# Value storage by head pair, a weight reload moved behind attention, and respaced conditioning and down weights in a two-layer decoder trunk

## The chip, the cores and the metric

The kernel runs as one program on all 8 cores of one Trainium2 chip. Each core computes one batch element, and the cores exchange nothing. The time of a run is that of the slowest core, in device microseconds (us). TensorE is written PE, VectorE DVE, ScalarE ACT, GpSimd POOL and SyncE SP; "SPq" and "ACTq" in a trace are the DMA-issuing instructions of SyncE and ScalarE.

The runs come in two states here. In the slow state the cores of one die (cores 0 to 3 are one, 4 to 7 the other), or of both, show a lower granted TensorE clock in the records and the run is some per cent longer. Measures used below:

- Fast runs: those within 1.5% of the fastest run of the same kernel. A ratio sets one kernel's fast runs against the other's fast runs of the same rounds, so it is not quite the ratio of the medians that are quoted.
- Undisturbed dies: where a kernel had too few fast runs, the mean core span over all dies whose four cores had a clock of at least 0.969, against the same mean of the kernel before in the same rounds. A run that is slow because of one die still gives one such die. The spans of such dies scatter within a kernel (standard deviation 3 to 17 us), so a difference by this measure is uncertain by some 3 to 8 us (standard error).
- Stages: cuts of a trace, explained with the profile.

## The reference, cut to what matters

```python
for l in range(DEPTH):                      # 2 layers, SEQ 4096, D_MODEL 1024, D_FF 2816
    mod = silu(c) @ ada_w[l] + ada_b[l]     # "conditioning": 9 x 1024 shifts, scales, gates
    y = modulate(rmsnorm(h, ...), sh1, sc1)
    h = h + 0.5 * g1 * swiglu(y, ffn1_wg, ffn1_wu, ffn1_wd)
    y = modulate(rmsnorm(h, ...), sh2, sc2)
    proj = y @ w_in[l]                      # u, v of the gating unit; q, k, v of attention
    out_a = spatial_gating(u, v, ...)
    out_b = dilated_mixture(rope(q), rope(k), v)   # 8 heads of 64
    h = h + g2 * (concat(out_a, out_b) @ w_out[l])
    y = modulate(rmsnorm(h, ...), sh3, sc3)
    h = h + 0.5 * g3 * swiglu(y, ffn2_wg, ffn2_wu, ffn2_wd)
```

`dilated_mixture` runs three causal patterns, (window, dilation) = (128, 1), (512, 4) and (2048, 16). For a dilation r, keys and values are taken at positions r apart, so their rows are not neighbours in memory.

## The kernel before

A sequence is cut in 8 tiles of 512 positions. Per layer the order on TensorE is: two feed-forward groups of two tiles each (gate and up matmuls, then down), projection 1 (tiles 0 to 3), two groups, with attention 1 running beside them, projection 2, output projection 1, two groups with attention 2 beside them, output projection 2, and two last groups. Everything that isn't the main line (attention, norms, conditioning, weight conversion, preparation) is a Python generator in a `Mix`. After each block of main matmuls `tick` adds its estimated nanoseconds to every generator's account, and each generator adds instructions until its own yields have used that account. So a yield of 5500.0 means "one piece per 5.5 us of main work". `drain` puts what is left of a generator into the program at once.

The background is thus interleaved when the program is built, into one list for each engine. The trace shows the result: from 1590.8 to 1603.5 us on core 4, in output projection 1, groups of 8 or 16 output-projection matmuls (L1326) alternate with groups of 8 of attention (L1173, L1202). SyncE's list alone is sorted once more, by the time at which a transfer's buffers are expected to be ready.

```python
class Mix:
    def tick(self, ns):
        for s in list(self.sides):
            s[1] += ns
            s[1] = min(s[1], 12000.0)
            while s[1] > 0 and s in self.sides:
                try:
                    s[1] -= next(s[0])
                except StopIteration:
                    self.sides.remove(s)
# ... cut ...
    def order_sp(self):
        for _, _, deps, fn, key in sorted(self.spq, key=lambda x: x[:2]):   # (ready, program order)
# ... cut ...
        def ada_gen(lo, cols, cost):            # conditioning, one 128-wide column of ada_w per piece
            ring = Zone(lo, B1).ring(8, [128, KC, 128], BF16, "ada")
            # ... cut ...
            for i, col in enumerate(cols):
                if i + n - 1 < len(cols):
                    load(i + n - 1)             # 256 KB by GpSimd's queue
                # ... cut ...
                ada_mm(ap, b, col)
                # ... cut ...
                yield cost
# ... cut ...
        def norm_load(t, src, bsrc):            # the residual tile, in four pieces
            for q in range(4):
                Sx.dma("sp", "h%d" % q, lambda e, q=q: e.dma_start(out=hbuf[0][:, 2 * q:2 * q + 2], in_=src[t, :, 2 * q:2 * q + 2]),
                       reads=bsrc[t][2 * q:2 * q + 2], writes=hbuf[1][2 * q:2 * q + 2])
# ... cut: projection, a value tile is stored ...
                vdst = bass.AP(vS.tensor, vS.offset + r0 * VW, [[VW, 16], [16 * VW, 8], [1, VW]])   # VW = 768: 1536 bytes
                Sx.dma("act", "va%d" % n, lambda e: e.dma_start(
                    out=vdst, in_=va.rearrange("p a c -> p (a c)")), reads=[bva], ...)
# ... cut: attention, the values of head pair p at dilation r ...
            def load_v(p, r):
                if r == 1:
                    # ... one DMA: 128 x 16 or 17 rows of 192 values (384 bytes) ...
                    return
                v, b = ax.v4 if r == 4 else ax.v16
                st_ = 128 * r
                n0 = -1 if sbi else 0
                for n in range(n0, SB // st_):
                    src = bass.AP(vS.tensor, vS.offset + (T0 + n * st_) * VW + p * 192,
                                  [[r * VW, 128], [VW, r], [1, 192]])
                    Sx.dma("sp", "av%d" % r, lambda e, n=n, src=src: e.dma_start(out=v[:, (n + 1) * r:(n + 2) * r, :], in_=src), ...)
# ... cut: output projection, the norm of a finished tile ...
                    def fin(sq=sq, t=t, n=n):
                        # ... cut ...
                        yield from norm_mods(1800.0, yv[ym[n // 2]], l, 2, t)
                        if n == 0:
                            norm_load(tiles[2], hS, bHS)
# ... cut: main line, projection 1 to output projection 1 ...
            side["at"] = mix.add(attn_gen(0, 1950.0))
            ffn_group(l, 0, (4, 5), src, bsrc, FB4, nxt=[f1(6), f1(7)])
            side["late"] = False
            def mid1(p, k):
                nonlocal mx
                if p == "down" and k == 4:
                    mix.drain(side["at"])                # the rest of attention 1, at once
                    mx = side["mx"] = MX()
                    # ... rope tables ...
                    side["win"] = mix.add(win_again(l, mx, 2200.0))   # projection weights again
            # ... cut ...
            ffn_group(l, 0, (6, 7), src, bsrc, FB4, posts=posts, hook=mid1)
            mix.drain(side["win"])
            project(4, False)
            # ... cut ...
            side["at"] = attn_gen(1, 2000.0)
```

The softmax here doesn't subtract the row's maximum and nothing guards it: scores larger than these inputs give would overflow.

## Time and profile before

Six runs of the kernel before gave a median of 5517.65 us (5323.34 to 6093.05), slow ones among them.

I cut the trace at the first matmul of each stage: gate (L733), down (L779), projection (L941), output projection (L1326 before, L1319 after). Attention is L1173 and L1202 before, L1166 and L1195 after. The matmuls that sum squares for a norm are L621. G is a gate stage and D a down stage with the group's number (8 groups in a layer), P a projection, O an output projection; P1 is the projection that follows group 1, O3 the output projection that comes after group 3 and projection P3. An undisturbed gate stage takes 152 us, a down stage 76 and an output projection 58 to 59. The first lines of the profile's page, which is of the slowest core:

```profile
span 5324.4 us, 84020 instructions; the slowest of 8 cores (5276.9 to 5324.4 us)
...
PE 4982.1 (94%) x27826; PEld 2323.7 (44%) x27826; DVE 2298.2 (43%) x4018; ACT 1895.3 (36%) x2879; POOL 664.4 (12%) x705
...
DMA packets 420054, 875.29 MB, mean 164 GB/s; under 512 B 154640, under 2 KB 187792, under 8 KB 412432
...
PE 75%; DMA 10%; ACT 6%; DVE 3%; issue 3%; SPq 2%; POOL 1%; ACTq 0%; DVEq 0%; POOLq 0%
```

TensorE is busy 94% of the span, and the chain that ended last (the last line) is 75% TensorE. So the kernel is near its bound, and what is left is a set of local stalls. They are seen in the windows of core 4, below in the order G0, D0, G1, D1, P1, D3 (the down stage that ends attention 1), O3 (output projection 1), O13 (output projection 2 of layer 1). The columns are the stage's start and end, its length, busy time and instructions of each engine, granted TensorE clock, share of the 16 DMA engines' time that was busy, and what they moved.

```profile
core 4: us, PE busy (x) PEld busy (x) DVE busy (x) ACT busy (x) POOL busy (x), PEclk, DMA share, GB/s
49.20:239.40 190.20, 174.72 (x961) 78.25 (x962) 73.40 (x112) 58.32 (x92) 29.61 (x56) 0.95 0.88 157
239.40:362.60 123.20, 87.72 (x474) 39.04 (x473) 18.64 (x28) 12.28 (x19) 16.94 (x32) 0.86 1.02 222
362.60:521.20 158.60, 155.31 (x802) 70.91 (x801) 62.98 (x97) 28.31 (x47) 15.33 (x29) 1.00 0.92 211
521.20:602.00 80.80, 79.71 (x369) 35.95 (x368) 22.50 (x33) 21.97 (x36) 2.64 (x5) 1.00 0.85 224
602.00:761.90 159.90, 152.57 (x738) 69.63 (x737) 105.93 (x301) 79.90 (x150) 92.97 (x74) 0.98 0.52 152
1235.70:1357.70 122.00, 91.65 (x492) 42.70 (x490) 32.17 (x51) 26.27 (x40) 11.72 (x12) 0.86 0.71 198
1519.80:1603.40 83.60, 66.90 (x377) 30.55 (x377) 38.48 (x57) 33.87 (x49) 0.20 (x1) 0.90 0.96 291
...
4760.70:4819.90 59.20, 58.86 (x274) 26.54 (x273) 33.87 (x49) 23.60 (x36) 0.00 (x0) 1.00 0.83 260
```

D0 is 47 us longer than an undisturbed down stage, with PE idle for 35.5 us (123.20 less 87.72) while the DMA engines are full (1.02). In G0 the DMA share is 0.88 and PE is busy for 174.7 of 190.2 us, so that stage has some DMA room. D3 has 30 us without a matmul, at a clock of 0.86. O3 has 16.7 us.

The waits of PE on core 4 say for what it stood still: us in all, number of times, longest.

```profile
PE ps L621 <- ACT arena L613: 74.7, 12, 18.2
...
PE ps L779 <- DMA arena<-wdS: 60.2, 5, 23.9
...
PE ps L733 <- DVE arena L792: 9.1, 2, 8.4
```

The first line is the norm of a residual tile that arrives late (L613 squares the tile's elements); one of its waits is in O3. The second is down weights, and its longest wait is in D3. The chain of work through O3 (start, us, what) shows why the tile was late there:

```profile
1536.45 0.32 SPq L1104
1537.07 0.59 SPq L1115
1537.76 10.96 SPq L1123
...
1562.92 7.36 DMA arena<-hS
1570.45 0.76 DVE arena L1334
1571.29 0.64 ACT arena L613
```

SyncE issues the K load of attention 2 (L1104), the dilation-1 value load (L1115) and then the first dilated one (L1123), and that one issue takes 10.96 us. Stores and the residual tile stand behind it in SyncE's list: the seven dilated loads take 19.79 us to issue, the next store goes at 1557.7 and the tile's load at 1562.9. All dilated value loads, and the value stores, in the trace of core 4 (issue duration in ns: least, median, most):

```profile
L1123 SPq DMA_DIRECT2D arena<-vS x96: 523/631/10964, 763.1 to 4552.1; - x96
...
L1043 ACTq DMA_DIRECT2D vS<-arena x64: 525/525/3777, 632.4 to 4112.7; - x64
```

### The profile page before, as it was taken

To read this page: it belongs to the slowest core of one execution; us is meant where nothing else is said; L and a number is where in the kernel's file an instruction comes from. 1 tells how busy PE (TensorE), PEld (TensorE's weight loads), DVE (VectorE), ACT (ScalarE), POOL (GpSimd) and SP (SyncE) were. 2 spreads that over 40 slices of the span, in tenths; PEclk is the share of its full clock that TensorE was granted. 3 is DMA by queue.
4 is the path that set the end of the run, shared out by engine and by line. 5 is a ranking of instruction groups with operands and counts; after the bars stand their busy time and mean duration, and the time that the engine had idled before them with its cause. 6 is when DMAs were issued, how large, how long until landed. Compare 5 with 4: busy or idle time off the path is not lost.

```text
span 5324.4 us, 84020 instructions; the slowest of 8 cores (5276.9 to 5324.4 us)
## 1 busy us (share of the span) xinstructions
PE 4982.1 (94%) x27826; PEld 2323.7 (44%) x27826; DVE 2298.2 (43%) x4018; ACT 1895.3 (36%) x2879; POOL 664.4 (12%) x705
## 2 busy tenths in 40 slices
PE   5969999998889999898999999999989999999998
PEld 2434444444334444344444444444444444444443
DVE  2313365443455544332333335544536544535342
ACT  2211253553334543112122313455424454513321
POOL 1110250011320011010100003300005000000000
PEclk9989999999999999899999999999999999999999
DMA  9898754644686554868676644546354736468331
GB/s 169 159 217 202 190 164 120 196 115 121 185 218 187 161 168 118 243 155 207 146 198 171 185 147 128 141 127 185 100 184 134 247 101 200 158 192 262 109 106 59
DMA packets 420054, 875.29 MB, mean 164 GB/s; under 512 B 154640, under 2 KB 187792, under 8 KB 412432
## 3 DMA queue, kind: packets, MB, share of 16 engines
q1 hardware_dynamic: 305392, 600.51, 36.1%
q0 software_dynamic: 40512, 139.35, 16.4%
q10 hardware_dynamic: 73728, 130.06, 7.6%
q8 instruction: 234, 3.83, 0.3%
q14 instruction: 188, 1.54, 0.1%
HBM read 821.94 MB, written 239.08 MB: 199 GB/s over the span
## 4 chain that ended last, share of the span: by engine, by line
PE 75%; DMA 10%; ACT 6%; DVE 3%; issue 3%; SPq 2%; POOL 1%; ACTq 0%; DVEq 0%; POOLq 0%
PE ps L733 42%; PE ps L779 18%; PE ps L941 6%; PE ps L1326 3%; PE ps L1202 3%; PE ps L1173 2%; DMA arena<-wd 2%; PE ps L621 2%; DMA arena<-wdS 1%; DMA arena<-wgu 1%; DMA hS<-arena 1%; DMA arena<-hS 1%; DMA arena<-xP 1%; POOL arena L1023 1%; DVE arena L1013 1%
## 5 line engine op out<-in xcount | busy, mean ns | idle before, releaser
L733 PE MATMUL ps<-arena 128*128 128x512 bf16 x11264 | 2568.8, 381 | 36.5 <-DMA arena<-wgu 11.4
L733 PEld LDWEIGHTS ps<-arena 128*128 128x128 bf16 x11264 | 1066.0, 98 | 1269.0 <-issue 75.2
L779 PE MATMUL ps<-arena 128*128 128x512 bf16 x5632 | 1289.8, 385 | 96.2 <-DMA arena<-wdS 50.1
L741 DVE SCALAR_TENSOR_TENSOR arena<-arena,ps 128x512 f32<-128x512 f32 x704 | 482.5, 685 | 1063.0 <-ACT arena L738 1047.0
L738 ACT ACTIVATE arena<-ps 128x512 f32<-128x512 f32 x704 | 419.3, 597 | 1429.2 <-PE ps L733 1187.6
L779 PEld LDWEIGHTS ps<-arena 128*128 128x128 bf16 x5632 | 543.7, 99 | 741.6 <-issue 135.2
L743 DVE TENSOR_TENSOR arena<-ps,arena 128x512 bf16<-128x512 f32 x704 | 486.8, 691 | 292.9 <-PE ps L733 256.5
L792 DVE SCALAR_TENSOR_TENSOR arena<-ps,arena 128x512 f32<-128x512 f32 x256 | 192.0, 750 | 945.3 <-PE ps L779 628.6
L941 PE MATMUL ps<-arena 128*128 128x512 bf16 x2560 | 579.8, 384 | 19.8 <-DVE arena L1013 16.7
L1180 ACT ACTIVATE arena<-ps 128x1024 bf16<-128x1024 f32 (+1 forms) x384 | 358.4, 933 | 382.0 <-PE ps L1173 357.7
L613 ACT ACTIVATE arena<-arena 128x512 bf16<-128x512 f32 x352 | 204.9, 625 | 597.1 <-DVE arena L1334 249.5
L941 PEld LDWEIGHTS ps<-arena 128*128 128x128 bf16 x2560 | 249.2, 99 | 316.4 <-issue 34.3
L645 ACT ACTIVATE arena<-arena 128x512 bf16<-128x512 f32 x384 | 257.1, 718 | 199.9 <-DVE arena L641 174.3
L1187 DVE TENSOR_TENSOR arena<-arena 128x1024 bf16<-128x1024 bf16 (+1 forms) x384 | 243.7, 635 | 125.9 <-ACT arena L1180 121.7
L641 DVE SCALAR_TENSOR_TENSOR arena<-arena,ps 128x512 f32<-128x512 f32 x384 | 263.2, 740 | 77.7 <-ACT ps L627 77.2
L1235 POOL TENSOR_TENSOR arena<-arena 64x512 bf16<-64x512 f32 x128 | 162.1, 1266 | 982.3 <-ACT arena L1231 935.8
L1023 POOL TENSOR_TENSOR arena<-arena 128x512 bf16<-128x512 f32 x128 | 226.7, 1876 | 285.3 <-DVE arena L1013 285.3
L1202 PE MATMUL ps<-arena 128*128 128x128 bf16 x2736 | 218.9, 221 | 40.1 <-ACT arena L1211 26.9
L1202 PEld LDWEIGHTS ps<-arena 128*128 128x128 bf16 x2736 | 184.9, 99 | 134.5 <-issue 51.9
L1326 PE MATMUL ps<-arena 128*128 128x512 bf16 x1024 | 238.9, 386 | 1.7 <-DVE arena L1061 1.7
L621 PE MATMUL ps<-arena 128*128 128x512 bf16 x448 | 148.2, 396 | 94.2 <-ACT arena L613 80.9
L1218 DVE TENSOR_TENSOR arena<-ps,arena 128x512 f32<-128x512 f32 x256 | 176.0, 687 | 104.8 <-PE ps L1202 103.9
(65 smaller groups left out, 2040.0 us busy)
## 6 DMA issues: line engine op xcount, KB each, us to landing
arena<-wguS SPq DMA_DIRECT2D x308, 512.0 KB, 4.1
arena<-hS SPq DMA_DIRECT2D x176, 512.0 KB, 7.2
arena<-wdS SPq DMA_DIRECT2D x112, 704.0 KB, 6.1
hS<-arena ACTq DMA_DIRECT2D x224, 256.0 KB, 6.3
arena<-hS ACTq DMA_DIRECT2D x160, 256.0 KB, 6.4
wguS<-wgu POOLq DMA_DIRECT2D x66, 512.0 KB, 6.9
hS<-arena SPq DMA_DIRECT2D x128, 256.0 KB, 9.1
arena<-ada_w POOLq DMA_DIRECT2D x120, 256.0 KB, 8.9
```

What stands on the lines that cost most here:

```text
L641: Sx.op("dve", lambda e: e.scalar_tensor_tensor(out=hk, in0=hk, scalar=Av[:, b0:b0 + 1], in1=bank(nb), op0=ALU.mult, op1=ALU.mult), reads= ...
L645: Sx.op("act", lambda e: e.activation(out=out, in_=hk, func=AF.Identity, bias=modv[:, s0:s0 + 1], scale=1.0), reads=[bh, bMod[l][i]], writ ...
L733: Sx.op("pe", lambda e, kc=kc, half=half, bk=bk: e.matmul(bank(bk), lhsT=gu[:, half, kc, :], rhs=y[:, kc, :], start=(kc == 0), stop=(kc == ...
L738: Sx.op("act", lambda e: e.activation(out=sg, in_=bank(G), func=AF.Tanh, scale=0.5), reads=[psB[G]], writes=[bsg])
L741: Sx.op("dve", lambda e: e.scalar_tensor_tensor(out=sg, in0=sg, scalar=1.0, in1=bank(G), op0=ALU.add, op1=ALU.mult), reads=[psB[G]], write ...
L743: Sx.op("dve", lambda e: e.tensor_tensor(out=fx.act[s][0][:, j, :], in0=bank(U), in1=sg, op=ALU.mult), reads=[psB[U], bsg], writes=[fx.act ...
L779: Sx.op("pe", lambda e, j=j: e.matmul(bank(bk), lhsT=wd[:, j, :], rhs=act[:, j, :], start=(j == 0), stop=(j == FC - 1)), reads=[bwd, ba[j] ...
L941: Sx.op("pe", lambda e, kc=kc, lhs=lhs, rhs=rhs: e.matmul(bank(bk), lhsT=lhs, rhs=rhs, start=(kc == 0), stop=(kc == KC - 1)), reads=[bw[c ...
L1023: Sx.op("pool", lambda e, o=o, a0=a0, a1=a1, h_=h_: e.tensor_tensor(out=cust(o, 0, to), in0=cust(a0[0], 0, fr), in1=cust(a1[0], 0, fr), op ...
L1180: Sx.op("act", lambda e: e.activation(out=pv, in_=ps[:, QB:QB + 2, c0:512], func=AF.Exp, scale=0.125), reads=[psB[QB], psB[QB + 1]], write ...
L1202: Sx.op("pe", lambda e, v=v, vi=vi, h=h, b=b, pc=pc, o=o, prev=prev: e.matmul(o, lhsT=v[:, vi, h * 64:h * 64 + 128], rhs=pT[:, h, pc, b, : ...
L1326: Sx.op("pe", lambda e, kc=kc, m=m, bk=bk, mxt=mxt: e.matmul(bank(bk), lhsT=ox.w[0][:, m, kc, :], rhs=mxt[:, kc, :], start=(kc == 0), stop ...
```

## The change

The intent, in five parts:

1. Values are stored by head pair (`vS` becomes `[4, S, 192]`), so that the r rows of one residue step are one long row: 1536 bytes at dilation 4, 6144 at dilation 16. One load replaces up to five. Each value tile is then stored with four DMAs of 384-byte rows, by SyncE, where it was one of 1536-byte rows by ScalarE.
2. In output projections the third tile's residual load goes on ScalarE's queue.
3. Attention 1 is spaced more densely, and the reload of the projection weights follows it in the same stream, in place of the forced `drain` in the middle of D3.
4. Attention 2 is spaced more densely, so that it ends earlier.
5. Conditioning takes one column every 7.2 us in place of 5.5, and down weights are opened at gate step 6 in place of 11.

```diff
-VW = 768
+VW = 192
-    vS = dscr("vS", [S, VW], BF16)
+    vS = dscr("vS", [4, S, VW], BF16)
@@ norm_load
-        def norm_load(t, src, bsrc):
+        def norm_load(t, src, bsrc, eng="sp"):
-                Sx.dma("sp", "h%d" % q, ...
+                Sx.dma(eng, "h%d" % q, ...
@@ vapart
-                vdst = bass.AP(vS.tensor, vS.offset + r0 * VW, [[VW, 16], [16 * VW, 8], [1, VW]])
-                Sx.dma("act", "va%d" % n, ...
+                for p in range(4):
+                    vdst = bass.AP(vS.tensor, vS.offset + (p * S + r0) * VW, [[VW, 16], [16 * VW, 8], [1, VW]])
+                    Sx.dma("sp", "va%d" % n, lambda e, p=p, vdst=vdst: e.dma_start(out=vdst, in_=va[:, p, :]), ...
@@ load_v   (the branch for r == 1 and the loop over n are gone)
+                v, b = {1: ax.v1, 4: ax.v4, 16: ax.v16}[r]
                 n0 = -1 if sbi else 0
+                n = SB // (128 * r) - n0
+                src = bass.AP(vS.tensor, vS.offset + (p * S + T0 + n0 * 128 * r) * VW,
+                              [[r * VW, 128], [128 * r * VW, n], [1, r * VW]])
+                Sx.dma("sp", "av%d" % r, lambda e: e.dma_start(out=v[:, (n0 + 1) * r:], in_=src), ...
@@ outproj
-                            norm_load(tiles[2], hS, bHS)
+                            norm_load(tiles[2], hS, bHS, "act")
@@ early, hook0
-                yield from ada_gen(mx.lo, list(range(24, 72)), 5500.0)
+                yield from ada_gen(mx.lo, list(range(24, 72)), 7200.0)
-                if n == 11:
+                if n == 6:
                     W.open_wd(4)
@@ main line   (mid1 and the drain in it are gone)
-            side["at"] = mix.add(attn_gen(0, 1950.0))
+            def prep1():
+                # ... new MX, rope tables ...
+                yield from win_again(l, mx, 2500.0)
+            side["late"] = False
+            side["at"] = mix.add(seq(attn_gen(0, 1800.0), prep1()))
-            ffn_group(l, 0, (6, 7), src, bsrc, FB4, posts=posts, hook=mid1)
-            mix.drain(side["win"])
+            ffn_group(l, 0, (6, 7), src, bsrc, FB4, posts=posts)
+            mix.drain(side["at"])
-            side["at"] = attn_gen(1, 2000.0)
+            side["at"] = attn_gen(1, 1850.0)
```

More of the change, by code (lines that the diff above doesn't have):

```diff
@@ L596, in conv_gen @@
                 yield cost
-        def norm_load(t, src, bsrc):
+        def norm_load(t, src, bsrc, eng="sp"):
             for q in range(4):
-                Sx.dma("sp", "h%d" % q, lambda e, q=q: e.dma_start(out=hbuf[0][:, 2 * q:2 * q + 2], in_=src[t, :, 2 * q:2 * q + 2]),
+                Sx.dma(eng, "h%d" % q, lambda e, q=q: e.dma_start(out=hbuf[0][:, 2 * q:2 * q + 2], in_=src[t, :, 2 * q:2 * q + 2]),
                        reads=bsrc[t][2 * q:2 * q + 2], writes=hbuf[1][2 * q:2 * q + 2])
@@ L1041, in vapart @@
                 r0 = t * T + s * 128
-                vdst = bass.AP(vS.tensor, vS.offset + r0 * VW, [[VW, 16], [16 * VW, 8], [1, VW]])
-                Sx.dma("act", "va%d" % n, lambda e: e.dma_start(
-                    out=vdst, in_=va.rearrange("p a c -> p (a c)")), reads=[bva],
-                    writes=[bVS[t]] if s == 0 else (), accw=[bVS[t]] if s else ())
+                for p in range(4):
+                    vdst = bass.AP(vS.tensor, vS.offset + (p * S + r0) * VW, [[VW, 16], [16 * VW, 8], [1, VW]])
+                    f = s == 0 and p == 0
+                    Sx.dma("sp", "va%d" % n, lambda e, p=p, vdst=vdst: e.dma_start(out=vdst, in_=va[:, p, :]), reads=[bva],
+                           writes=[bVS[t]] if f else (), accw=() if f else [bVS[t]], ns=500.0)
                 tick(KC * MM)
@@ L1109, in load_v @@
                 rd = [bVS[t] for t in tp]
-                if r == 1:
-                    v, b = ax.v1
-                    lo = 0 if sbi else 1
-                    r0 = T0 + (lo - 1) * 128
-                    src = bass.AP(vS.tensor, vS.offset + r0 * VW + p * 192, [[VW, 128], [128 * VW, 17 - lo], [1, 192]])
-                    Sx.dma("sp", "av1", lambda e: e.dma_start(out=v[:, lo:17, :], in_=src), reads=rd, writes=[b], ns=6000.0)
-                    return
-                v, b = ax.v4 if r == 4 else ax.v16
-                st_ = 128 * r
-                n0 = -1 if sbi else 0
-                for n in range(n0, SB // st_):
-                    src = bass.AP(vS.tensor, vS.offset + (T0 + n * st_) * VW + p * 192,
-                                  [[r * VW, 128], [VW, r], [1, 192]])
-                    Sx.dma("sp", "av%d" % r, lambda e, n=n, src=src: e.dma_start(out=v[:, (n + 1) * r:(n + 2) * r, :], in_=src),
-                           reads=rd, writes=[b] if n == n0 else (), accw=() if n == n0 else [b], ns=1500.0 * r / 4)
+                v, b = {1: ax.v1, 4: ax.v4, 16: ax.v16}[r]
+                n0 = -1 if sbi else 0
+                n = SB // (128 * r) - n0
+                src = bass.AP(vS.tensor, vS.offset + (p * S + T0 + n0 * 128 * r) * VW,
+                              [[r * VW, 128], [128 * r * VW, n], [1, r * VW]])
+                Sx.dma("sp", "av%d" % r, lambda e: e.dma_start(out=v[:, (n0 + 1) * r:], in_=src), reads=rd, writes=[b],
+                       ns=4000.0)
             BACK = {1: 128, 4: 512, 16: 2048}
@@ L1482, in build_nc @@
             project(0, True)
-            side["at"] = mix.add(attn_gen(0, 1950.0))
-            ffn_group(l, 0, (4, 5), src, bsrc, FB4, nxt=[f1(6), f1(7)])
-            side["late"] = False
-            def mid1(p, k):
-                nonlocal mx
-                if p == "down" and k == 4:
-                    mix.drain(side["at"])
-                    mx = side["mx"] = MX()
-                    mx.late()
-                    side["late"] = True
-                    load_cs(mx, 4)
-                    load_cs(mx, 5)
-                    side["win"] = mix.add(win_again(l, mx, 2200.0))
+            def prep1():
+                nonlocal mx
+                mx = side["mx"] = MX()
+                mx.late()
+                side["late"] = True
+                load_cs(mx, 4)
+                load_cs(mx, 5)
+                yield from win_again(l, mx, 2500.0)
+            side["late"] = False
+            side["at"] = mix.add(seq(attn_gen(0, 1800.0), prep1()))
+            ffn_group(l, 0, (4, 5), src, bsrc, FB4, nxt=[f1(6), f1(7)])
             posts = seq(*[norm_steps(2200.0, (lambda k=k: mx.y2[k]), *p2(4 + k), gate=lambda: side["late"], lead=14000.0)
```

## The prediction

> All times are of fast runs: before takes 5324 us (the 5518 median includes slow ones).
>
> **What bounds it.** TensorE is busy 94% of the span (page part 1) and 75% of the chain of waits; the rest is local stalls. Cutting the trace at the first matmul of each gate (L733), down (L779), projection (L941) and output-projection (L1326) stage, an undisturbed gate takes 152 us, a down 76, an output projection about 58. Excess, layer 0 / layer 1:
> - start: first gate 194, first down 128 us (24, 10 and 3 us idle on wd; DMA share 1.03);
> - the down that ends attention 1: 123 / 109 us (forced attention tail 12 us, then 16 us on wdS, issued late);
> - output projection after it: 84 / 79 us (16.5 / 12.4 us idle for an hS tile queued behind value loads, one of whose issues took 10.1 / 8.2 us, timeline);
> - the down that ends attention 2: 97 / 86 us (17 / 5 us on wdS), then an output projection of 70 / 59.
> After idling, matmuls go at 427 ns instead of 215 for some us; granted clock 0.84 to 0.92 here. [...] each cured stall saves some us extra.
>
> **What the change does.**
> 1. Values: dilated loads go from 384-byte rows to 1536 and 6144; stores become 256 of 384-byte rows on SyncE instead of 64 of 1536 on ScalarE. [...] packets of 384, 1536 and 4096 bytes take 24, 79 and 205 ns, about equal per byte. So transfers save an estimated 25 us of all-engine time, less 9 for stores, none critical. Issuing counts: dilated loads cost SyncE 115 us.
> 2. Residual tile loads on ScalarE's queue, not stuck behind those. 1 and 2 together: about -12 us in each first output projection, -8 in layer 0's second.
> 3. Attention 7.5% denser, weights reloaded from its stream: no forced tail, wd less blocked: -22 and -12.
> 4. Attention 2 ends in the gate stage (instruction order), so output weights arrive earlier: -17 and -8.
> 5. Conditioning every 7.2 instead of 5.5 us: 36 instead of 44 columns used by the end of the first down (2 MB less in a DMA-bound stretch), -10; wd opened at step 6 only moves a wait. But conditioning now ends late in the second down; the order has eight norm matmuls at its end: a new stall of about 10 us before the projection.
> Costs: denser attention, more SyncE issues in projections, +5.
>
> Sum about -95: 5230 us, 1.8% faster. Range 5165 to 5285. Faster by over 2% 0.38, within 2% 0.58, slower 0.04.
>
> **What shows it.** Down ending attention 1 about 100 us; first output projections about 70; down ending attention 2 about 78; first gate plus down about 310; second down about 95 with an idle stretch before L941; packets under 512 bytes 154640 to about 101000; dilated value issues on SyncE from 115 us to under 20.
>
> **What would make it wrong.** A start deeper in DMA debt could gain much more; the win reload could still crowd wdS loads, since rope loads still wait ahead of them on SyncE; value stores could delay norm tiles in projections; the stall before the first projection could be 20 us.

Two clauses are cut from it, at the marks. No term of the sum was in them: it came to about -95 us and stays so.

## The result, and the profile after

The changed kernel took 5322.45 us in the median of 20 runs (5306.21 to 6067.06); the kernel before 5341.75 in the median of 40 (5315.85 to 6103.82). Of fast runs alone the medians are 5320.0 (13 runs) and 5325.0 (21 runs). The ratio of fast runs, computed as said above, is 0.9986, with a 95% interval of 0.9976 to 0.9996. Outputs are right. So the change is worth 0.14%, where 1.8% had been predicted, and the time lies above the predicted range.

Two lines of the page after:

```profile
span 5335.5 us, 84085 instructions; the slowest of 8 cores (5259.9 to 5335.5 us)
...
DMA packets 372951, 875.31 MB, mean 164 GB/s; under 512 B 103440, under 2 KB 137616, under 8 KB 365328
```

Bytes are the same, and a third of the packets under 512 bytes is gone: the store and load forms did change as meant. The windows of core 4 after, in the order of those before:

```profile
core 4: us, PE busy (x) PEld busy (x) DVE busy (x) ACT busy (x) POOL busy (x), PEclk, DMA share, GB/s
49.50:241.40 191.90, 174.12 (x921) 77.07 (x922) 72.92 (x111) 57.82 (x91) 26.97 (x51) 0.95 0.83 150
241.40:363.40 122.00, 87.29 (x449) 38.84 (x448) 19.15 (x29) 12.88 (x20) 15.85 (x30) 0.85 1.03 221
363.40:529.30 165.90, 160.08 (x865) 73.67 (x866) 61.33 (x92) 27.55 (x45) 19.02 (x36) 0.97 0.89 191
529.30:621.40 92.10, 82.14 (x370) 36.15 (x369) 19.87 (x30) 16.84 (x27) 5.40 (x9) 0.94 0.88 248
621.40:795.40 174.00, 156.87 (x738) 70.69 (x737) 111.00 (x308) 86.32 (x159) 90.06 (x70) 0.95 0.47 127
1273.10:1379.20 106.10, 83.28 (x404) 37.64 (x402) 24.37 (x37) 21.03 (x33) 12.54 (x13) 0.89 0.81 228
1540.60:1625.10 84.50, 68.93 (x384) 31.49 (x385) 38.77 (x57) 34.33 (x50) 0.51 (x1) 0.92 0.95 276
...
4759.00:4824.20 65.20, 60.53 (x273) 26.78 (x272) 33.76 (x49) 24.86 (x37) 0.00 (x0) 0.97 0.77 251
```

G0 and D0 are as long as before. G1, D1 and P1 are 7, 11 and 14 us longer: by the end of P1 the core is 33.5 us late (795.4 against 761.9). D3 is 16 us shorter. O3 hasn't gained. O13, which had stood still for nothing, is 6 us longer.

All stages of the span, as the mean over the six cores whose matmul records are complete in both traces (1, 2, 3, 4, 5 and 7; both runs fast), in us. Stage times of the experiments are such means too, less the mean before of this table; in four of them (two-speed conditioning, conditioning back, attention with residual, late attention) the complete cores are 0, 1, 3, 5, 6 and 7:

| stage | before | after | difference |
|---|---|---|---|
| G0 and D0 | 315.3 | 312.9 | -2.4 |
| G1 and D1 | 241.9 | 263.7 | +21.8 |
| P1 | 159.8 | 174.2 | +14.4 |
| D3 / D11 (end of attention 1, layers 0 / 1) | 120.8 / 107.4 | 103.5 / 86.2 | -17.3 / -21.3 |
| O3 / O11 (output projection 1) | 82.0 / 79.5 | 80.6 / 78.0 | -1.4 / -1.5 |
| G4, D4, G5 / G12, D12, G13 (attention 2 beside) | 473.5 / 478.5 | 482.1 / 482.5 | +8.6 / +4.0 |
| G2, D2, G3 / G10, D10, G11 (attention 1 beside) | 473.8 / 476.2 | 476.2 / 477.2 | +2.4 / +1.0 |
| D5 / D13 (end of attention 2) | 93.6 / 84.2 | 87.7 / 77.4 | -5.9 / -6.8 |
| O5 / O13 (output projection 2) | 69.2 / 59.4 | 67.5 / 65.9 | -1.7 / +6.4 |
| all other stages and the ends | | | -2.0 |
| span | 5302.9 | 5301.2 | -1.7 |

One of these six cores was disturbed: in the changed kernel's trace the clock record of core 1 stood at 0.8125 from 376.9 to 508.7 us, in its G1, which took 192.2 us (164.6 to 167.0 on the other five). With core 1 left out of both means, G1 and D1 differ by +17.8, G0 to P1 in all by +31.2, and the span by -7.7, near the 0.14%; the other rows move by 1.5 us at most.

The gain did come, and was given back: -55.9 us from D3 and D11 (-38.6), D5 and D13 (-12.7), O3 and O11 (-2.9) and O5 (-1.7); against it +33.8 at the start, +6.4 in O13 and +16.0 in the stages with attention beside them. What PE waited for after:

```profile
PE ps L621 <- ACT arena L613: 67.1, 17, 17.1
PE ps L779 <- DMA arena<-wdS: 40.1, 3, 22.8
PE ps L733 <- DVE arena L792: 26.4, 3, 11.3
```

The waits on down weights fell by 20 us, but the longest one, in D3, is there as before (22.8 us). The gate stages' wait on L792, the add of the down result to the residual, rose from 9.1 to 26.4 us. Two places show the start's loss. The end of D1 (timeline: start, us, what, and in brackets how long the engine had been idle and what ended it):

```profile
604.16 3.19 PE L779 MATMUL ps<-arena 128*128 128x512 bf16 x14
...
609.56 4.93 SPq L601 DMA_DIRECT2D arena<-hS  x4
...
615.56 1.15 ACT L613 ACTIVATE arena<-arena 128x512 bf16<-128x512 f32 x2 [1.52 <-DMA arena<-hS]
...
616.45 1.01 PE L621 MATMUL ps<-arena 128*128 128x512 bf16 x2 [9.10 <-ACT arena L613]
```

The last down matmul ends at 607.4; the residual tile for the next norm is asked for at 609.6, when the previous norm has freed its buffer; and PE stands until 616.4, since the projection needs that norm. These norms are held back in the program until conditioning and the gating unit's preparation are done. In the order of instructions the last conditioning matmul stood at gate matmul 304 of 704 of G1 before, and stands at 672 after; so the norms begin later, and the second tile's eight norm matmuls now stand behind the last down matmul of D1. The other place is the start of G1:

```profile
363.41 3.57 PE L733 MATMUL ps<-arena 128*128 128x512 bf16 x8 [9.30 <-DVE arena L792]
...
371.89 0.75 DVE L792 SCALAR_TENSOR_TENSOR arena<-ps,arena 128x512 f32<-128x512 f32 x1 [8.63 <-DMA arena<-xP]
```

PE waits for a residual add that waits for a tile of the input x. The eight matmuls after the wait take 3.57 us, 446 ns each: twice the usual 215.

The chain through O3 after:

```profile
1553.48 11.79 DMA kS<-arena
1565.40 0.32 SPq L1105
1566.01 0.46 SPq L1116
1566.57 11.37 SPq L1116
...
1587.43 18.36 DMA arena<-mS
```

The long issue is still there: 11.37 us, though it is now one of the new long-row loads (L1116 is `load_v` for every dilation). And all of it stands later in the stage: the K load (L1105) is issued 24.8 us after the stage's start (1565.4 less 1540.6) and was at 16.7 us before (1536.5 less 1519.8). It waits for the last K store. SyncE's timeline has that store at 1552.8, 12.2 us after the start of O3, where it was at 1524.6, 4.8 us after it; SyncE now issues the sixteen value stores of a tile between the K stores, from 1534.7 to 1547.0. So 7.4 of the 8.1 us by which the K load is later are already in the K store. The value issues after, core 4:

```profile
L1116 SPq DMA_DIRECT2D arena<-vS x48: 319/371/13590, 801.6 to 4532.6; - x48
...
L1045 SPq DMA_DIRECT2D vS<-arena x256: 517/592/6404, 652.8 to 4127.7; - x128
```

Summed over the trace of core 4, value loads cost SyncE 60 us of issuing after and 119 us before. But the stores cost it 176 us, and cost ScalarE 37 us before. SyncE's issues in all rose from 753 to 878 us.

### The profile page after: what moved, and what is told of

Read it like the earlier page. It is cut to its first block, busy times and chain, and to the rows that moved or that the text cites. A ratio compares the mean times of both kernels' runs of the same rounds, so it can differ in the third digit from the quotient of the medians.

```text
span 5335.5 us, 84085 instructions; the slowest of 8 cores (5259.9 to 5335.5 us)
## 1 busy us (share of the span) xinstructions
PE 5004.7 (94%) x27826; PEld 2328.1 (44%) x27826; DVE 2301.0 (43%) x4018; ACT 1903.9 (36%) x2883; POOL 666.1 (12%) x705
## 2 busy tenths in 40 slices
DMA packets 372951, 875.31 MB, mean 164 GB/s; under 512 B 103440, under 2 KB 137616, under 8 KB 365328
## 4 chain that ended last, share of the span: by engine, by line
PE 75%; DMA 10%; ACT 6%; DVE 3%; issue 3%; POOL 2%; SPq 1%; ACTq 0%; DVEq 0%; POOLq 0%
PE ps L733 43%; PE ps L779 17%; PE ps L941 5%; DMA hS<-arena 3%; PE ps L1195 3%; PE ps L1319 2%; PE ps L1166 2%; DMA arena<-xP 2%; PE ps L621 1%; DMA arena<-hS 1%; DMA arena<-wdS 1%; POOL arena L1023 1%; DVE arena L1013 1%; ACT arena L645 1%; DVE arena L641 1%
## 5 line engine op out<-in xcount | busy, mean ns | idle before, releaser
L779 PE MATMUL ps<-arena 128*128 128x512 bf16 x5632 | 1275.9, 382 | 73.1 <-DMA arena<-wdS 41.3
L941 PE MATMUL ps<-arena 128*128 128x512 bf16 x2560 | 582.4, 385 | 27.7 <-DVE arena L1013 22.5
L792 DVE SCALAR_TENSOR_TENSOR arena<-ps,arena 128x512 f32<-128x512 f32 x256 | 192.1, 750 | 912.3 <-PE ps L779 613.6
L645 ACT ACTIVATE arena<-arena 128x512 bf16<-128x512 f32 x384 | 259.6, 721 | 208.0 <-DVE arena L641 189.9
L641 DVE SCALAR_TENSOR_TENSOR arena<-arena,ps 128x512 f32<-128x512 f32 x384 | 263.9, 741 | 95.1 <-ACT ps L627 82.4
```

What stands on the lines that cost most here:

```text
L641: Sx.op("dve", lambda e: e.scalar_tensor_tensor(out=hk, in0=hk, scalar=Av[:, b0:b0 + 1], in1=bank(nb), op0=ALU.mult, op1=ALU.mult), reads= ...
L645: Sx.op("act", lambda e: e.activation(out=out, in_=hk, func=AF.Identity, bias=modv[:, s0:s0 + 1], scale=1.0), reads=[bh, bMod[l][i]], writ ...
L779: Sx.op("pe", lambda e, j=j: e.matmul(bank(bk), lhsT=wd[:, j, :], rhs=act[:, j, :], start=(j == 0), stop=(j == FC - 1)), reads=[bwd, ba[j] ...
L941: Sx.op("pe", lambda e, kc=kc, lhs=lhs, rhs=rhs: e.matmul(bank(bk), lhsT=lhs, rhs=rhs, start=(kc == 0), stop=(kc == KC - 1)), reads=[bw[c ...
```

## The experiments

Twelve kernels ran, all with right outputs. The first four undo nothing: each is the kernel before with one part of the change.

Theory: the start alone (part 5) costs some 35 us, and the other parts gain nearly what it costs. A first rival: the parts hurt each other, the value stores and the denser attention above all, and the start is only where it shows. A second: the new value layout is by itself what costs the time.

### The start alone

```diff
-                yield from ada_gen(mx.lo, list(range(24, 72)), 5500.0)
+                yield from ada_gen(mx.lo, list(range(24, 72)), 7200.0)
-                if n == 11:
+                if n == 6:
```

> Before with only the two respacings at the start (conditioning every 7.2 us instead of 5.5, wd opened at step 6). Theory A, conditioning that ends late: the second gate and down stages together cost about 22 us more (241.9 to 264, mean of the six cores with complete records), with a stretch of 8 to 9 us idle on a norm matmul at the end of the down stage, and the projection after it 14 us more (159.8 to 174); the first gate plus down stay within 4 us; all in all +33 us, ratio 1.006. Rival B, the loss comes from the value stores moved to SyncE, or only in company with them: the projection stays at 160, and all in all at most +10.

Measured: 5362.46 us in the median, ratio 1.007 (1.0047 to 1.0092); on undisturbed dies 5342.1 us against 5299.5, +42.6. G1 and D1 grew by 17.9 us and P1 by 13.8, near the whole change's 17.8 (core 1 left out) and 14.4; G0 and D0 fell by 5.5. So the loss at the start belongs to part 5 and needs none of the other parts. In this trace it is 26.2 of the 32.4 us by which the span grew.

### Values alone

The edit is that of `VW`, `vS`, `vapart` and `load_v` in the diff above.

> Before with only the value layout (stores and loads). Theory A: the projections move by 3 us at most (first one stays at 160), the first output projections by 4 us at most, total within 8 us of before, ratio 0.999 to 1.0015: the rows' length is off the critical path and the SyncE time saved on loads is spent on stores. Rival B (value stores on SyncE spoil the projection): first projection +10 us or more. Rival C (long rows free the hS tile in the first output projections, as I predicted): those fall by 5 us or more each.

Measured: its seven runs (5360.77 to 6125.64 us) had too few fast ones for a ratio. On undisturbed dies it took 5301.3 us, +1.8. On cores 1 to 3, which were undisturbed in the profile, O3 took 87.2 us, 5.2 more than before, O11 1.9 more, and D11 7.0 less. So by itself the new layout gives nothing and costs almost nothing; the second rival falls.

### Attention and the reload alone

The edit is the main-line part of the diff (`prep1`, 1800.0, 1850.0, without `mid1`).

> Before with only the denser attention and the mixer weights reloaded from its stream. Theory: the down stages that end attention 1 fall by 17 and 21 us (120.8 to 104, 107.4 to 86), those that end attention 2 by 6 and 7; the attention stages after the first output projections rise by up to 8 and 4 us; the output projection of layer 1's second half stays at 59.4. All in all -42 us, ratio 0.992. Rival: these gains need the value layout or the residual loads on ScalarE, and half of them or less appear here.

Measured: ratio 0.9924 (0.9898 to 0.9951), the fast runs at 5281.4 and 5283.35 us; on undisturbed dies -44.5 us. D3 took 96.4 us (-24.5) and D11 86.0 (-21.5). By the two ratios (0.9924 and 0.9986) this one part alone, without the rest, is 0.6% faster than the whole change. The price of the density is seen beside it: G4 to G5 took 6.0 us more and G12 to G13 3.8.

### The residual load alone

```diff
-        def norm_load(t, src, bsrc):
+        def norm_load(t, src, bsrc, eng="sp"):
...
-                            norm_load(tiles[2], hS, bHS)
+                            norm_load(tiles[2], hS, bHS, "act")
```

> Before with only the residual tile loads of the output projections on ScalarE's queue. Theory A: layer 1's second output projection, which lost nothing before, rises by 6 us (59.4 to 65.5), as the issue now stands behind ScalarE's other work; the first output projections fall by 5 to 10 us each because the hS tile is no longer behind the value loads on SyncE. Rival B: the tile is late through DMA bandwidth, not through its place in a queue; then the first output projections stay within 3 us of 82 and 79.5.

Measured: one fast run, 5316.89 us, so no ratio; on undisturbed dies -9.0 us. O3 gained 4.5 us and O11 6.2. O13 lost 7.2. There SyncE had issued the four pieces one by one as their buffers came free, at 4785.3 to 4792.5 us in the kernel before; ScalarE, in the whole change, issues all four only at 4788.6 to 4790.7, behind its own activations.

The four parts together make +42.6 + 1.8 - 44.5 - 9.0 = -9.1 us on undisturbed dies. The whole change's 0.14% is some 7 us. The sum is uncertain by some 13 us. Within that the parts add up, so the first rival falls too: no cost much larger than that comes from their meeting.

### Conditioning back to 5.5 us, the rest of the change kept

```diff
-                yield from ada_gen(mx.lo, list(range(24, 72)), 7200.0)
+                yield from ada_gen(mx.lo, list(range(24, 72)), 5500.0)
```

> The changed kernel with conditioning back to every 5.5 us; wd still opens at step 6. Theory A (conditioning that ends late costs the 36 us): second gate plus down back from 263.7 to about 243, first projection back from 174.2 to 160, mean span of the six complete cores back from 5301 to about 5267; ratio to before 0.993. Rival B (opening wd earlier does it): both stay as in the changed kernel, ratio 0.9985.

Measured: one fast run, 5324.35 us, in which die 0 had a lower clock (0.970 to 0.976 against 0.977 to 0.981); no ratio. On undisturbed dies -37.0 us against the kernel before. G1 and D1 were at +2.1 and P1 at +0.3 us (G0 and D0 at +12.0, but the clock record of cores 0 and 1 stood at 0.8125 for over 200 us there; on cores 4 to 7 G0 and D0 took 2.4 us more than on the same cores before). So what G1, D1 and P1 had lost, 32.1 us without core 1, is the price of the 7.2, all but 2.4 us. Down weights at step 6 are in this kernel too, so they do no harm in those stages. For G0 and D0 that isn't settled: step 6 never ran alone, and the other kernel with step 6 and 5.5 us (the dilation-1 load last, below), whose trace has no such clock, stands at +6.6 there.

### Conditioning at two speeds

If the loss is only that conditioning ends late, it should vanish when its second half is quick.

```diff
-        def ada_gen(lo, cols, cost):
+        def ada_gen(lo, cols, cost, late=None):
...
-                yield cost
+                yield cost if late is None or i < 24 else late
...
-                yield from ada_gen(mx.lo, list(range(24, 72)), 7200.0)
+                yield from ada_gen(mx.lo, list(range(24, 72)), 7200.0, 3000.0)
```

> The changed kernel with conditioning at 7.2 us for its first 24 columns and 3.0 us for the other 24, so that it ends as early in the second gate stage as before (288 of 704 matmuls; before 304), but still leaves the first gate stage the same room on the DMA queues. Theory A, lateness: no idle stretch of 9 us at the end of the second down stage, and the projection is back at 160; the stall of up to 15 us at the start of the second gate stage, on residual tiles, may stay, so second gate plus down 245 to 255; ratio 0.993 to 0.995. Rival C, the slower pace itself in the first gate stage does the harm: projection stays above 170.

Measured: four runs of 5306.37 to 5325.98 us, all fast, no ratio given; on undisturbed dies -32.0 us. G1, D1 and P1 of its core 5, the columns as in the windows above:

```profile
359.10:530.20 171.10, 162.88 (x839) 73.95 (x840) 63.25 (x98) 31.70 (x53) 16.38 (x31) 0.96 0.91 199
530.20:611.40 81.20, 78.97 (x364) 35.21 (x363) 22.22 (x32) 18.82 (x29) 2.64 (x5) 1.00 0.86 231
611.40:773.90 162.50, 152.37 (x737) 69.55 (x736) 106.13 (x301) 79.68 (x149) 92.94 (x74) 0.98 0.54 148
```

D1 and P1 are back (81.2 and 162.5 us), so their loss was the late end of conditioning. G1 is not: 171.1 us. Its wait on residual adds comes right at its start, here as in the whole change and in the start alone, and not with conditioning back at 5.5 us. That loss belongs to the slow first half.

### Attention, with the residual load on ScalarE in the first output projections only

```diff
-                            norm_load(tiles[2], hS, bHS)
+                            norm_load(tiles[2], hS, bHS, "sp" if tiles[0] else "act")
```

This is on top of the attention part.

> The version that I put together from the single runs: before, plus the denser attention with its reload, plus the residual tile on ScalarE's queue only in the first output projection of each layer. If the parts add: -45 from attention, -4.5 and -6 in the two first output projections, nothing in the others: mean span 5303 - 55 = 5248, ratio 0.990. Against the run with conditioning back it tells the value layout in company: if that is neutral, the two differ only by the 6 us of the last output projection; rival, the layout gives back part of the gains (down stage ending attention 1 at 103 instead of 96, first output projections at 80 instead of 77 and 73): then 15 us or more.

Measured: its lowest two runs were 5282.53 and 5313.07 us, no ratio; on undisturbed dies -48.7 us. O3 took 77.1 (-4.9) and O11 73.1 (-6.4), and O13 was at 59.4 us as before. So the loss in O13 was the queue, and can be had back by keeping SyncE there. In O3 PE waited up to 6.3 us for the norm and then, on seven of the eight cores, 3.8 to 10.4 for the tile of mixer outputs (`mS`): the wait had moved.

### The mixer-output tiles on ScalarE too

```diff
-                    load_mx(ox, n, tiles[n + 2])
+                    load_mx(ox, n, tiles[n + 2], "sp" if tiles[0] else "act")
```

This is on top of the last one; `load_mx` got an engine argument.

> The version with attention and residual parts, plus the mixed tile (mS) of the first output projection of each layer on ScalarE's queue too, so that nothing which that stage waits for stands behind the value loads on SyncE. Theory F, place in SyncE's queue: the idle stretch of 4 to 5 us on mS goes, first output projections 77.1 and 73.1 to about 71 and 68. Rival D, DMA bandwidth: the tile lands no earlier, both stay within 2 us. Total 5 to 12 us below that version under F; about 0.989 of before.

Measured: median 5287.21 us, ratio 0.9903 (0.9884 to 0.9923), the lowest ratio of all kernels; on undisturbed dies -57.9. But O3 took 78.0 us and O11 73.4, no less than without it (77.1 and 73.1). The tile's place in SyncE's queue had made it late: on cores 1, 5 and 7 the second `mS` load is now issued 32 to 37 us after the start of O3, where it was 47 to 51, and PE's wait for it is gone from O3 on all eight cores. But the stage was no shorter, for other waits came in its place; on six cores an attention matmul now waited 1.9 to 9.6 us for ScalarE's exponentials (0.9 at most without this edit). SyncE's timeline in O3 of core 5 shows what still stands in its list:

```profile
1542.28 31.23 SPq L1123 DMA_DIRECT2D arena<-vS  x7
1573.66 6.72 SPq L1338 DMA_DIRECT2D hS<-arena  x8
```

The stores of finished residual tiles (`hS`) wait behind seven value-load issues, and the norm's multiply (L641), which overwrites the stored tile, waits for a store. So with the other issuer the tile was issued some 15 us earlier and the stage was no shorter: 78.0 us against 77.1, at a DMA share of 0.98 (core 4; 0.98 on core 5 without this edit).

### Attention 2 started later

```diff
-            side["at"] = attn_gen(1, 1850.0)
+            side["at"] = seq(pause(52000.0), attn_gen(1, 1750.0))
```

This is on top of the attention-and-residual kernel, to take attention 2's loads out of the output projection.

> The version above with the loads and first units of attention 2 put off until the first output projection is over (52 us of matmul time; attention paced at 1.75 us so that it still ends before the output weights are wanted). Theory D, that output projection is bound by DMA bandwidth (its DMA share is 0.97 to 0.99): it falls from 77 and 73 to 66 or less, against about 6 us that leave it as attention matmuls; the following gate stages rise by up to 8 us. Rival E, bandwidth is not the limit: it falls by 6 us or less (71 and 67). Total against the version above: -10 to +8 us under either, as attention 2 is now denser and may run into the down stage.

Measured: one fast run, 5318.49 us; on undisturbed dies -25.2 us. It missed its aim. SyncE's list is sorted by when buffers are ready, and the loads' buffers were, so they were still issued inside the stage (in O11 from 4081 to 4100 us). Only the attention itself came later, and G4 to G5 cost 24.0 us more. O3 took 75.4 us and O11 70.4 (77.1 and 73.1 with attention in it): with the loads still inside, taking the attention matmuls out gave 1.7 and 2.7 us.

### Attention 2's loads really held

The edit adds `floor=bool(sbi)` to the q, k and value loads, so that attention 2's are sorted no earlier than the matmul that precedes them in the program. It is on top of the previous one.

> What the late-attention run failed to do (its value loads still went out inside the output projection, as SyncE's list is sorted by when the buffers are free): the first loads of attention 2 are held on SyncE until after the first output projection; mixed tile on SyncE as in the version above it. Theory F or D both predict that the stage falls to 62 to 66 us with under 4 us idle. If it stays above 70, the stage waits for something else than the value loads. The gate stages after it wait for the q, k and v tiles in exchange: G4 to G5 +5 to +25 us, so the total is no better than the version without it.

Measured: ratio 0.9935 (0.9904 to 0.9967); on undisturbed dies -39.9 us. O3 and G4 of its core 5:

```profile
1517.20:1581.90 64.70, 59.02 (x272) 26.61 (x273) 33.75 (x49) 24.42 (x37) 0.22 (x1) 1.00 0.89 278
1581.90:1784.30 202.40, 191.48 (x1282) 93.19 (x1281) 95.33 (x144) 97.51 (x132) 12.58 (x13) 0.97 0.54 156
```

On the six cores O3 fell to 63.7 and O11 to 62.8 us, the only kernel in which the first output projections come near their 58 to 59. G4 to G5 took 25.6 us more and G12 to G13 15.0, so most of it was given back. The run before is the clean comparison, since it too has no attention matmuls in these stages: against its 75.4 and 70.4 us, the loads alone are 11.7 us of O3 and 7.6 of O11. How they cost it is not settled. With them gone the stage still moves 278 GB/s on core 5, near the 287 of core 5 in the attention-and-residual kernel, with them in the stage, which points to DMA time; but they also leave SyncE's list, in which other transfers stood behind them, and the two were not parted.

### Loads held by half

```diff
-            side["at"] = attn_gen(1, 1850.0)
+            side["at"] = seq(pause(24000.0), attn_gen(1, 1850.0))
```

This is on top of the kernel with mixer-output tiles on ScalarE, with the same `floor`.

> A try for a better version: attention part, residual and mixed tile on ScalarE's queue, and the first loads of attention 2 held back by 24 us of matmul time instead of 52, so that they follow the hS and mixed tiles of the first output projection, with attention still paced at 1.85 us. If the bytes only have to move out of the first half of that stage: output projections 78 and 73 to 66 to 70, the gate stages after them up by no more than 4 us, total 6 to 14 us below the version without the hold (5257 mean of undisturbed dies, 0.990), so 0.988. If, as in the run with loads held for the whole stage, what the stage gives is taken back after it (there -14 and -10, then +17 and +10), the total stays within 4 us of 0.990.

Measured: ratio 0.9928 (0.9859 to 0.9997); on undisturbed dies -31.3 us. O3 took 81.4 us, with a wait of 7.4 to 13.2 us of an attention matmul on ScalarE's exponentials. The trace of core 5 shows its cause: the exponential stands in ScalarE's list behind a norm instruction (L645), that one waits for VectorE's L641, and L641 waits for a store of the residual tile that SyncE issued behind seven dilated value loads, which took 23.7 us to issue. The loads, held for 24 us, had come just in front of these stores. No better middle was found here.

### The dilation-1 load last

Which load does the 11 us issue belong to? If the cause is the dilation-1 load with its 384-byte rows, the block should follow that load wherever it stands.

```diff
-            for r in (1, 4, 16):
+            for r in (16, 4, 1):
                 load_v(0, r)
```

This is on top of the kernel with conditioning back at 5.5 us.

> The changed kernel with conditioning back at 5.5 us (run of that name), and the first value loads of each attention in the order dilation 16, 4, 1 instead of 1, 4, 16. Theory G: the 8 to 14 us issue on SyncE that I expected long rows to end belongs to whatever is issued behind the dilation-1 load, whose 2048 or 2176 rows of 384 bytes the change leaves as they are; then with that load last the dilated value issues take under 1 us each there, the value issues all together fall from 56 to under 15 us per core, and the block shows at the next issue on SyncE. Rival H: SyncE blocks because all DMA engines are busy there, whatever stands behind what: then one of the value issues still takes over 5 us at each of the two starts of attention 2.

Measured: ratio 0.994 (0.9917 to 0.9963); on undisturbed dies -42.6 us. SyncE in O3, core 5 (timeline):

```profile
1514.88 4.36 SPq L1116 DMA_DIRECT2D arena<-vS  x3
1519.39 22.14 SPq L1331 DMA_DIRECT2D hS<-arena  x4
```

Three value loads are issued in 4.36 us, where three took 14.45 us in the changed kernel (1566.0 to 1580.5 on core 4). The four stores behind them now take 22.14 us, though they are the same plain stores as always. On all eight cores the issue next behind the dilation-1 load took 17.7 to 22.8 us in O3 and 14.0 to 21.8 in O11; in the changed kernel that next issue is the dilation-4 load, with 9.2 to 13.8 and 8.1 to 13.6. So the block belongs to whatever is issued behind the dilation-1 load, which has 128 x 16 (attention 1) or 128 x 17 rows of 384 bytes (attention 2) in both kernels: the change never shortened it. It isn't the whole of it: standing last, the dilation-1 load itself took 2.2 to 5.6 us to issue in O3 and 4.1 to 10.0 in O11, where it takes 0.4 to 0.6 standing first. Value-load issues in all fell to 29 to 34 us a core (expected: under 15), from 49 to 58 without the swap, and the time that was saved there was lost on other issues: O3 stayed at 80.7 us (80.0 without) and O11 at 77.0 (78.2).

## Why the prediction was wrong

It was wrong on the time: 5320 us in the median of fast runs, 90 above the 5230 predicted and 35 above the range's upper end. "Within 2%" had been given 0.58. The terms of the prediction add up to -96 us (steps 1 and 2 -32, step 3 -34, step 4 -25, step 5 -10, costs +5). By the stage table the same terms measured +1.8 (with O13), -38.6, -12.7, +33.8 and +16.0. So of the 96 us that are missing, 44 are step 5's (41 without core 1), 34 those of steps 1 and 2, 12 step 4's and 11 the costs'; step 3 gave 5 more than predicted. Point by point:

- **Step 5, the start, is the step that failed most.** "Conditioning every 7.2 instead of 5.5 us: 36 instead of 44 columns used by the end of the first down (2 MB less in a DMA-bound stretch), -10" with "a new stall of about 10 us before the projection": only the -10 is in the sum of -95, the stall is named and not counted. It measured +33.8 us over G0 to P1 (+31.2 without core 1). Three things went wrong in it.
  - The -10: the bytes did fall, but not where DMA was the limit. By the windows of core 4 (length times GB/s), G0 moved 29.9 MB before and 28.8 after, and D0 27.4 and 27.0. The saving is 1.5 MB, 1.1 of it in G0, whose DMA share merely fell from 0.88 to 0.83. D0 stayed full (1.02 and 1.03) and as long as it was: PE stood still for 35.5 us in it before and for 34.7 after. (Against the two kernels with step 6 and 5.5 us, at +2.4 and +6.6 us in G0 and D0, the 7.2 does gain a few us there; step 6 alone was not run.)
  - The stall before the projection was predicted at 10 us and was there: 9.1 us on core 4. What wasn't foreseen is what follows it. P1 grew by 14.4 us: the clock record around the stall stood at 0.50 from 609.5 us for 13.7 us, and again for 6.8 us from 657.3 in P1, where PE stood still for 17.1 us (7.3 before), 4.6 of them in one wait. Running conditioning quickly in its second half gave D1 and P1 back.
  - G1's 7.7 us (core 1 left out; 7.3 on core 4) were not foreseen at all: after, the residual adds wait for input tiles as G1 starts (9.3 and 5.8 us on core 4). The wait that D0 had on weights has moved there. It stays when conditioning is slow only in its first half, and goes with 5.5 us. Which transfer pushes the input tiles back wasn't separated; that stays open.
- **Step 1, values.** The transfer side was right: packets under 512 bytes are 103440 (predicted "about 101000"), and on core 4 the time of value-size packets fell from 223 to 199 us of all engines (-24; estimated -16), none of it critical. Packets of 384 bytes took 24 ns there after the change (16 bytes per ns), of 1536 bytes 83 (18.4) and of 6144 bytes 273 (22.5), so the long rows did gain per byte, slowly. The issue side was wrong. "Dilated value issues on SyncE from 115 us to under 20" became 60 us for all value loads, because the 11 us issue isn't the dilated load's own; the swap of the load order shows that it comes behind the dilation-1 load. And 256 stores on SyncE cost it 176 us, which the prediction had lumped into "+5". On core 4 they delay the K stores, and with them the K load of attention 2, by 7 to 8 us.
- **Steps 1 and 2 in the output projections failed as well.** Predicted -12 in each first one and -8 in O5; measured -1.4, -1.5 and -1.7. The residual load alone gave -4.5 and -6.2, so the mechanism is real, at a third to a half of the size. Values alone added 5.2 and 1.9 us there, and the whole change with conditioning put back stood at 80.0 and 78.2 us where attention and residual without the values stood at 77.1 and 73.1: the values took most of it back. The rest could not be had by moving one tile to another queue: when the residual tile and then the `mS` tile left SyncE's list, the wait went to other transfers that still stood behind the value loads. Only with attention 2's loads out of the stage does it fall to 64 us, and the loads only move. "Value stores could delay norm tiles in projections" was on the list of what could go wrong; it was the K stores instead. The loss of 6.4 us in O13 was not foreseen: a load that SyncE issues in pieces as buffers come free was put behind ScalarE's activations.
- **Step 3, attention and reload, was right.** Predicted -22 and -12, measured -17.3 and -21.3. In the kernel before, the forced rest of attention was 11.5 us of attention matmuls alone (1264.2 to 1275.7 us on core 4). Part of the gain is work that moved: 88 of the 128 attention matmuls of D3 now stand in G2 to G3, which grew by 2.4 us. In layer 0 the wait on down weights stayed, 22.8 us against 23.9 before. The list's "the win reload could still crowd wdS loads" fits that (one of the reload's issues took 9.0 us in D3), but no run shows it.
- **Step 4 was right in direction, and its size was off:** -17 and -8 predicted, -5.9 and -6.8 measured. The base was partly at fault: I took D5 from the slowest core, 97 us, while the mean of the six cores is 93.6.
- **Costs.** Predicted +5, measured +16.0 in the stages beside attention. The attention part alone shows 9.8 of it (6.0 and 3.8), so the density costs something beside it, whatever it saves at its end. Part of that is again work that moved: G4 to G5 hold 24 attention matmuls more and D5 32 fewer, G12 to G13 40 more and D13 48 fewer. How much of the rest is waiting was not separated.
- **The clock.** In the record of core 4 it stood at 0.50 around the waits named here: at G1's start from 356.9 us for 10.2 us, and the eight matmuls after the 9.3 us wait took 446 ns each, where 215 is usual. "Each cured stall saves some us extra" fits D3, whose clock rose from 0.86 to 0.89 (the record at 0.50 for 34.1 us before, for 23.9 after), and its reverse, which I did not apply to my own new stall, fits D1 and P1, where it fell from 1.00 and 0.98 to 0.94 and 0.95 (core 4). How long a wait has to be for this was not measured. Nor does any run show why the slow state comes in some executions only: in the profiled run of values alone cores 4 to 7 had mean clocks of 0.914 to 0.920 and cores 0 to 3 0.974 to 0.980, with the same kernel.

The best kernel keeps the attention part, the residual and mixer tiles on ScalarE in first output projections only, the old value layout and the old start: ratio 0.9903 to the kernel before. It differs from the attention part alone (0.9924) by less than their intervals are wide.

## What to carry to other kernels

Before spacing background work further apart, check that its bytes leave the stretch in which DMA is full: here 1.1 of the 1.5 MB that left came from G0 (DMA share 0.88), and D0 (1.02) stayed as long as it was. The end of that work then comes later: look in the instruction order for what waits behind it (here 9.1 us before P1). When a change with several parts moves nothing, run the parts singly before explaining anything; here a loss of 43 us hid a gain of 45. Count the issues on both sides of a layout change, and ask whether a slow issue is slow by itself or stands behind another (four stores took 22.14 us here behind the dilation-1 load).
